# Differential attention: low parts of both maps made in one operation and moved by ScalarE; one maximum for two maps that share a bank

## The chip, the cores and the metric

The kernel runs on one core of a Trainium2 chip. The core has a matrix engine (TensorE, PE in the profile; its weight loads are shown apart as PEld), VectorE (DVE), ScalarE (ACT), GpSimd (POOL), and SyncE (SP), which issues most of the DMAs. Each engine works through its own queue in order; semaphores make one wait for another. SBUF is the on-chip memory; PSUM holds the results of matmuls in eight banks of 128 partitions x 512 f32. The metric is device time in microseconds (us) of one execution. Beside the timed runs there is one profiled execution, with the times of every instruction.

## The reference, cut to what matters

The model is a trunk of two layers, over 512 tokens of width 1024. Each layer has a half-step SwiGLU, a token mixer, a cross-attention into 256 memory tokens, and another half-step SwiGLU, each followed by a layer norm. The mixer of the first layer is the differential attention that the change touches: eight heads, each with two query/key pairs of 64 dimensions (the two "maps"), whose softmaxes are subtracted.

```python
q, k, v = jnp.split(x @ w_qkv, 3, axis=-1)
q = q.reshape(B, S, H, 2, dk)            # H = 8, dk = 64, S = 512
k = k.reshape(B, S, H, 2, dk)
v = v.reshape(B, S, H, 2 * dk)
q = rope(q, c5, s5)
k = rope(k, c5, s5)
...
s = jnp.einsum('bqhcd,bkhcd->bhcqk', qblk, k).astype(jnp.float32) * scale
s = jnp.where(mask, s, jnp.finfo(jnp.float32).min)
p = jax.nn.softmax(s, axis=-1)
a = p[:, :, 0] - lam * p[:, :, 1]
return jnp.einsum('bhqk,bkhe->bqhe', a.astype(v.dtype), v)
```

## The kernel before

Everything is f32. The matmuls take a reduced f32 type (`fp32r`), so each operand is cut in two: a high part, which is a cast by ACT (lines 119, 272, 1046), and a low part, which is what the cast lost, subtracted by DVE (lines 120, 274, 1047). A product is then three matmuls: high x high, high x low, low x high (lines 202 to 204).

**The attention stage.** `da_main` goes through the heads in pairs. For each pair it projects the values, and for each head of it the query and the key, as a tile of 128 rows (64 of the first map, 64 of the second) by 512 tokens. The weights come by DMA, are cut in two by ACT and DVE, and five buffers of each part hold them ahead of TensorE. Beside this main work runs a side chain, `da_side`, for each head and each block of 128 query tokens (i = 0 to 3; block i sees n = 128 (i + 1) keys): scores and softmax (`da_scores`); two steps later the transposes of the difference of the maps (`da_turn`, lines 482, 119, 120); three steps later the product with the values (`da_out`, lines 1092 and 1093), then the sums of squares (lines 1097 to 1101); and at the end of a head the scaling (line 1117, with a factor that POOL makes) and the turn of the output (`da_turn_out`, lines 124, 125). `weave` mixes the two in the order of the program: it counts nominal nanoseconds of the main work and takes a step of the side chain whenever enough have passed. A head's first scores may come 6000 nominal ns after its key's projection. The order on PE follows the program; on ACT and DVE a planner with a cost model may pull operations that are ready ahead of others.

**Query and key.** `da_rope` rotates the projected tile: DVE shuffles it into a tile `t2` (line 1019) and multiplies by the cosines into `t1` (1020), POOL multiplies `t2` by the sines (1021), DVE adds the two (1022). Both tiles are of the tag `rt`, which has two buffers. Then the high and low parts go to where the score matmuls want them. A query of map m is one tile of 128 rows: its high part in the 64 rows of the map, its low part in the other 64. `da_query` makes each half with operations on 64 rows: ACT makes the high part (1032), DVE the low part, written into the other rows (1033); twice each. A key has, for each map, a tile with the high part in both halves, and a tile with the low part in the map's half and zeros in the other. `da_key` makes for each map the high part by ACT (1046), the low part by DVE (1047), and copies the high part to the other half by ACT (1048).

**Scores.** For each map three matmuls go into a PSUM bank: query x high key (1061), query x low key (1062), and the causal mask (1063). Then DVE takes the maximum of each map's rows (1066), ACT exponentiates and sums (1067), DVE takes a reciprocal and a factor (1070, 1071) and subtracts the second map from the first (1072).

**Banks.** `aux` (line 186) gives a bank to each of these tiles (`sc` for scores, `pt` for transposes, `po` for outputs) from three names in rotation, with two buffers for each name, six banks in all; the other two belong to the projections. A tile waits until one of the two buffers of its name has been read to the end. In `da_side` a head draws 8 banks for scores, 4 for transposes, 2 for outputs and 1 for the output's turn, 15 in all.

Of the kernel before, what the change touches and what calls it, by code (L numbers as in the profile page):

```python
# [9 lines left out]
F32 = mybir.dt.float32  # L10
F32R = mybir.dt.float32r
I32 = mybir.dt.int32
AF = mybir.ActivationFunctionType
ALU = mybir.AluOpType
AX = mybir.AxisListType
# [4 lines left out]
S = 512  # L20
# [20 lines left out]
HALVES = (slice(0, DA_DK), slice(DA_DK, P))  # L41
# [68 lines left out]
class Trunk:  # L110
# [72 lines left out]
    def mm(self, name):  # L183
        return self.mmp.tile([P, S], F32, tag="mm", name=name)
# [840 lines left out]
    def da_query(self, ps):  # L1025

        nc, t = self.nc, self.da_rope(ps)
        got = [self.act("qk") for m in range(2)]
        scale = DA_DK**-0.5
        for m, q in enumerate(got):  # L1030
            here, there = HALVES[m], HALVES[1 - m]
            nc.scalar.activation(q[here], t[here], AF.Copy, scale=scale)
            nc.vector.scalar_tensor_tensor(
                q[there], t[here], scale, q[here].bitcast(F32), ALU.mult, ALU.subtract
            )
        return got

    def da_key(self, ps):


        nc, t = self.nc, self.da_rope(ps)
        his, los = [self.act("qk") for m in range(2)], self.low_keys[len(self.heads) % 2]
        for m in range(2):
            here, there = HALVES[m], HALVES[1 - m]
            hi, lo = his[m], los[m]
            nc.scalar.copy(hi[here], t[here])
            nc.vector.tensor_sub(lo[here], t[here], hi[here].bitcast(F32))
            nc.scalar.copy(hi[there], hi[here].bitcast(F32))
        return his, los

    def da_scores(self, st, i):

        nc = self.nc
        q, k, n = st["q"], st["k"], (i + 1) * P
        qi, kn = slice(i * P, n), slice(0, n)
        mx, rc, cf = self.small("mx"), self.small("rc", (P, 1)), self.small("cf", (P, 1))
        sm = st["sm"][:, i]
        sc = [self.aux("sc")[:, :n] for m in range(2)]
        mm = nc.tensor.matmul
        for m in range(2):  # L1060
            mm(sc[m], q[m][:, qi], k[0][m][:, kn], start=True, stop=False)
            mm(sc[m], q[m][:, qi], k[1][m][:, kn], start=False, stop=False)
            mm(sc[m][:, n - P :], self.identr, self.maskr, start=False, stop=True)
        p = [self.tmp("p")[:, :n] for m in range(2)]
        for m in range(2):
            nc.vector.tensor_reduce(mx[:, m : m + 1], sc[m], AX.X, ALU.max, negate=True)
            nc.scalar.activation(
                p[m], sc[m], AF.Exp, bias=mx[:, m : m + 1], accum_out=sm[:, m : m + 1]
            )
        nc.vector.reciprocal(rc, sm[:, 1:2])  # L1070
        nc.vector.scalar_tensor_tensor(cf, sm[:, 0:1], self.nlam, rc, ALU.mult, ALU.mult)
        nc.vector.scalar_tensor_tensor(p[0], p[1], cf, p[0], ALU.mult, ALU.add)
        st["p", i] = p[0]
# [512 lines left out]
```

## Time and profile before

| | us |
|---|---|
| median of the three runs | 1948.64 |
| lowest, highest run | 1948.03, 1959.1 |
| the profiled execution, its own time | 1954.6 |
| its span, from the first to the last instruction | 1952.8 |
| TensorE, VectorE, ScalarE, GpSimd busy | 1917.3, 1567.3, 1019.6, 323.2 |

The profiled execution took 6 us more than the median; durations below come from it. A row of an instruction gives its start in us from the span's start, its length in us, the engine, the line of the kernel, the operation, the tiles that it writes and reads, and, in brackets, how long its engine stood idle before it and what ended that. Matmuls overlap their neighbours, and their ends are modelled; the distance between two starts says more than the length shown. A row of a group gives the line, the engine, the operation, output and input tiles, their shape, the count, then the busy time in us and the mean ns of one, and the idle time before them. A row of a wait names who waited, for whom, the us in total, how often, and the longest. The granted clock of TensorE was 0.994 of full speed over the span.

### The profile page before, as it was taken

To read this page: it belongs to the slowest core of one execution; us is meant where nothing else is said; L and a number is where in the kernel's file an instruction comes from. 1 tells how busy PE (TensorE), PEld (TensorE's weight loads), DVE (VectorE), ACT (ScalarE), POOL (GpSimd) and SP (SyncE) were. 2 spreads that over 40 slices of the span, in tenths; PEclk is the share of its full clock that TensorE was granted. 3 is DMA by queue.
4 is the path that set the end of the run, shared out by engine and by line. 5 is a ranking of instruction groups with operands and counts; after the bars stand their busy time and mean duration, and the time that the engine had idled before them with its cause. 6 is when DMAs were issued, how large, how long until landed. Compare 5 with 4: busy or idle time off the path is not lost.

```text
span 1952.8 us, 32548 instructions
## 1 busy us (share of the span) xinstructions
PE 1917.3 (98%) x13122; PEld 1751.0 (90%) x13122; DVE 1567.3 (80%) x2214; ACT 1019.6 (52%) x1549; POOL 323.2 (17%) x299
## 2 busy tenths in 40 slices
PE   8999999999999999999999999999999999999998
PEld 8999998888778888999998999999888889999996
DVE  6898889788867557889887888888777559988886
ACT  6555454566655434655553655545445336555552
POOL 2112111111211002211220311212100003111211
PEclk9999999999999999999999999999989999999999
DMA  9878772322134316977785687877253338878861
GB/s 272 182 169 178 173 137 76 89 74 78 45 118 140 109 65 183 184 175 161 145 191 170 114 179 162 184 171 142 77 173 130 103 108 151 175 164 170 183 134 56
DMA packets 247031, 277.96 MB, mean 142 GB/s; under 512 B 8288, under 2 KB 212576, under 8 KB 246880
## 3 DMA queue, kind: packets, MB, share of 16 engines
q0 software_dynamic: 92928, 92.29, 30.9%
q1 hardware_dynamic: 153952, 183.59, 29.3%
q8 instruction: 103, 1.69, 0.3%
q14 instruction: 48, 0.39, 0.1%
HBM read 273.75 MB, written 2.10 MB: 141 GB/s over the span
## 4 chain that ended last, share of the span: by engine, by line
PE 50%; DVE 6%; issue 3%; ACT 1%; POOL 1%; DMA 0%; SPq 0%; DVEq 0%; POOLq 0%; ACTq 0%
PE x L202 5%; PE x L203 5%; PE x L204 5%; PE z L202 3%; PE z L204 3%; PE z L203 3%; PE ps L202 2%; PE ps L204 2%; PE ps L203 2%; PE px L202 2%; PE px L204 2%; PE px L203 2%; DVE wl L120 1%; PE y L204 1%; PE x L674 1%
## 5 line engine op out<-in xcount | busy, mean ns | idle before, releaser
L659 POOL DMA_DIRECT2D ra<-in_ffn_w_in_dram x132 | 170.4, 1304 | 996.2 <-DVE wl L120 819.6
L119 ACT CAST wh<-ra 128x1024 fp32r<-128x1024 f32 x184 | 193.5, 1053 | 224.3 <-PE x L203 65.3
L120 DVE TENSOR_TENSOR wl<-ra,wh 128x1024 fp32r<-128x1024 f32 x184 | 223.8, 1220 | 73.8 <-ACT wh L119 73.3
L119 ACT CAST wh<-rc 128x1024 fp32r<-128x1024 f32 x136 | 143.1, 1053 | 119.1 <-PE x L203 38.8
L202 PE MATMUL x<-xe,wh 128*128 128x256 f32 x704 | 195.0, 277 | 0.0
L203 PE MATMUL x<-xe,wh 128*128 128x256 f32 x704 | 194.8, 277 | 0.0
L204 PE MATMUL x<-xe,wl 128*128 128x256 f32 x704 | 194.8, 277 | 0.0
L120 DVE TENSOR_TENSOR wl<-rc,wh 128x1024 fp32r<-128x1024 f32 x136 | 164.6, 1219 | 28.5 <-ACT wh L119 28.0
L119 ACT CAST wh<-b 128x1024 fp32r<-128x1024 f32 x112 | 117.8, 1052 | 131.1 <-PE x L203 65.9
L120 DVE TENSOR_TENSOR wl<-b,wh 128x1024 fp32r<-128x1024 f32 x112 | 136.7, 1220 | 40.2 <-ACT wh L119 40.2
L202 PE MATMUL x<-xh,wh 128*128 128x256 f32 x544 | 151.2, 278 | 0.9 <-DVE hr L738 0.9
L203 PE MATMUL x<-xl,wh 128*128 128x256 f32 x544 | 150.7, 277 | 0.0
L204 PE MATMUL x<-xh,wl 128*128 128x256 f32 x544 | 150.7, 277 | 0.0
L203 PEld LDWEIGHTS x<-xe,wh 128*128 128x128 f32 x704 | 132.5, 188 | 1.4
L202 PEld LDWEIGHTS x<-xe,wh 128*128 128x128 f32 x704 | 132.1, 188 | 1.3
L204 PEld LDWEIGHTS x<-xe,wl 128*128 128x128 f32 x704 | 132.2, 188 | 0.0
L120 DVE TENSOR_TENSOR wl<-raw,wh 128x1024 fp32r<-128x1024 f32 x64 | 80.5, 1265 | 55.1 <-ACT wh L119 54.4
L202 PEld LDWEIGHTS x<-xh,wh 128*128 128x128 f32 x544 | 102.1, 188 | 1.8 <-issue 1.1
L203 PEld LDWEIGHTS x<-xl,wh 128*128 128x128 f32 x544 | 102.5, 188 | 0.7
L119 ACT CAST wh<-raw 128x1024 fp32r<-128x1024 f32 x64 | 66.6, 1049 | 69.2 <-PE xq L203 21.6
L204 PEld LDWEIGHTS x<-xh,wl 128*128 128x128 f32 x544 | 102.2, 188 | 0.0
L204 PE MATMUL y<-xh,wl 128*128 128x256 f32 x352 | 98.4, 280 | 1.5 <-DVE wl L120 0.3
(435 smaller groups left out, 6356.8 us busy)
## 6 DMA issues: line engine op xcount, KB each, us to landing
ra<-in_ffn_w_in_dram POOLq DMA_DIRECT2D x132, 512.0 KB, 6.9
rc<-in_ffn_w_in_dram SPq DMA_DIRECT2D x88, 512.0 KB, 5.9
b<-in_ffn_w_out_dram SPq DMA_DIRECT2D x76, 512.0 KB, 4.9
ra<-in_ffn_w_in_dram SPq DMA_DIRECT2D x44, 512.0 KB, 5.1
rc<-in_ffn_w_in_dram POOLq DMA_DIRECT2D x44, 512.0 KB, 7.8
raw<-in_xa_wkv_dram SPq DMA_DIRECT2D x16, 1024.0 KB, 5.4
raw<-in_da_w_qkv_dram SPq DMA_DIRECT2D x16, 512.0 KB, 5.1
raw<-in_xa_wq_dram SPq DMA_DIRECT2D x8, 1024.0 KB, 5.1
```

What stands on the lines that cost most here:

```text
L119: self.nc.scalar.copy(hi, src),
L120: self.nc.vector.tensor_sub(lo, src, hi.bitcast(F32)),
L202: mm(out, w[0], x[0], start=start, stop=False, skip_group_check=again)
L203: mm(out, w[0], x[1], start=False, stop=False, skip_group_check=again)
L204: self.last_mm = mm(out, w[1], x[0], start=False, stop=stop, skip_group_check=again)
L659: nc.gpsimd.dma_start(t, source(*block), accum_op=ALU.add)
L674: self.last_mm = nc.tensor.matmul(ps[:, j], v[i][:, k, j * P : (j + 1) * P], x[l][:, k], start=n == i == l == 0, stop=n == 7 and i == 1, s ...
```

## The change

A query's low part is made for both maps by one DVE operation of 128 rows, into a third tile of the tag `rt`, and so is its high part by one ACT operation. Three ACT copies of 64 rows then put the pieces where the matmuls want them: the second map's high part and both low parts. A key gets the same: one high part, one low part, then five ACT copies (three of high parts, two of low parts).

In `da_scores`, where both maps' scores fit into one bank (2n up to 512, so blocks 0 and 1), they share one, and DVE takes the maxima of both maps with one operation. A head draws 13 banks then. Blocks 2 and 3 stay as they are.

```diff
 def da_query(self, ps):
         nc, t = self.nc, self.da_rope(ps)
         got = [self.act("qk") for m in range(2)]
         scale = DA_DK**-0.5
-        for m, q in enumerate(got):
-            here, there = HALVES[m], HALVES[1 - m]
-            nc.scalar.activation(q[here], t[here], AF.Copy, scale=scale)
-            nc.vector.scalar_tensor_tensor(
-                q[there], t[here], scale, q[here].bitcast(F32), ALU.mult, ALU.subtract
-            )
+        low = self.tmp("rt")
+
+        self.split_scaled(got[0], low, t, scale)
+        nc.scalar.copy(got[1][HALVES[1]], got[0][HALVES[1]].bitcast(F32))
+        for m in range(2):
+            nc.scalar.copy(got[m][HALVES[1 - m]], low[HALVES[m]])
         return got
...
 def da_key(self, ps):
         his, los = [self.act("qk") for m in range(2)], self.low_keys[len(self.heads) % 2]
-        for m in range(2):
-            here, there = HALVES[m], HALVES[1 - m]
-            hi, lo = his[m], los[m]
-            nc.scalar.copy(hi[here], t[here])
-            nc.vector.tensor_sub(lo[here], t[here], hi[here].bitcast(F32))
-            nc.scalar.copy(hi[there], hi[here].bitcast(F32))
+        low = self.tmp("rt")
+        self.split(his[0], low, t)
+        for half in HALVES[::-1]:
+            nc.scalar.copy(his[1][half], his[0][HALVES[1]].bitcast(F32))
+        nc.scalar.copy(his[0][HALVES[1]], his[0][HALVES[0]].bitcast(F32))
+        for lo, half in zip(los, HALVES):
+            nc.scalar.copy(lo[half], low[half])
         return his, los
...
 def da_scores(self, st, i):
-        sc = [self.aux("sc")[:, :n] for m in range(2)]
+        both = 2 * n <= S
+        if both:
+            sc = self.aux("sc")[:, : 2 * n].rearrange("p (m n) -> p m n", m=2)
+            pair, sc = sc, [sc[:, m] for m in range(2)]
+        else:
+            sc = [self.aux("sc")[:, :n] for m in range(2)]
...
+        if both:
+            nc.vector.tensor_reduce(mx, pair, AX.X, ALU.max, negate=True)
         for m in range(2):
-            nc.vector.tensor_reduce(mx[:, m : m + 1], sc[m], AX.X, ALU.max, negate=True)
+            if not both:
+                nc.vector.tensor_reduce(mx[:, m : m + 1], sc[m], AX.X, ALU.max, negate=True)
             nc.scalar.activation(
```

## The prediction

> **What bounds the kernel now.** I read the page first, then the stage that the change touches, stretch by stretch, then the waits of TensorE in that stage.
>
> ```profile
> span 1952.8 us, 32548 instructions
> PE 1917.3 (98%) x13122; PEld 1751.0 (90%) x13122; DVE 1567.3 (80%) x2214; ACT 1019.6 (52%) x1549; POOL 323.2 (17%) x299
> ```
>
> The second row is busy time by engine over the whole span. TensorE (PE) is covered at 98%, VectorE (DVE) at 80%, ScalarE (ACT) at 52%. These are means over eight stages, so the attention stage is read by itself. Its head loop lies between 362 and 580 us. In the rows below the columns after the length are PE, PEld (weight loads), DVE, ACT and POOL in us busy, then the granted clock, DMA share and GB/s.
>
> ```profile
> 362.00:580.00 218.00, 213.20 (x1257) 177.89 (x1256) 176.86 (x372) 135.72 (x363) 35.89 (x48) 1.00 0.26 79
> ...
> 460.00:480.00 20.00, 19.61 (x104) 16.25 (x103) 17.99 (x38) 14.34 (x38) 5.48 (x7) 1.00 0.33 106
> 480.00:500.00 20.00, 18.36 (x98) 14.09 (x98) 15.88 (x36) 12.78 (x34) 4.26 (x6) 1.00 0.16 53
> 500.00:520.00 20.00, 18.64 (x106) 14.50 (x104) 16.90 (x34) 12.07 (x35) 5.60 (x7) 1.00 0.16 54
> 520.00:540.00 20.00, 19.70 (x145) 17.69 (x145) 16.87 (x39) 15.55 (x46) 2.05 (x4) 1.00 0.18 56
> ```
>
> TensorE is uncovered for 218.00 - 213.20 = 4.8 us of this stage, and 3.4 of those fall between 460 and 540 us, the later heads. That is all that a change of DVE and ACT work can win here, unless the covered time itself hides stalls. The starts of three neighbouring projection matmuls say that it mostly does not:
>
> ```profile
> 501.80 0.39 PE L202 MATMUL q<-xh,wh 128*128 128x512 f32 x1
> 502.04 0.39 PE L203 MATMUL q<-xl,wh 128*128 128x512 f32 x1
> 502.27 0.39 PE L204 MATMUL q<-xh,wl 128*128 128x512 f32 x1
> ```
>
> They start 0.23 to 0.24 us apart, although each is shown 0.39 long: an uninterrupted stream. So TensorE bounds the stage, and what counts is where it stops:
>
> ```profile
> PE sc L1061 <- DVE a L120: 1.7, 2, 1.3
> PE pt L482 <- ACT o L1117: 1.1, 1, 1.1
> PE po L1092 <- ACT a L119: 0.6, 1, 0.6
> PE sc L1061 <- ACT po L1101: 0.6, 1, 0.6
> PE po L1093 <- DVE a L120: 0.3, 1, 0.3
> PE pt L482 <- ACT p L1067: 0.2, 1, 0.2
> ```
>
> Columns: us in total, times, longest. The two `sc` rows, 1.7 + 0.6 = 2.3 us, are score matmuls that wait for a PSUM bank still being read. The largest one:
>
> ```profile
> 498.80 0.39 PE L1061 MATMUL sc<-qk 128*128 128x256 f32 x1 [1.31 <-DVE a L120]
> ```
>
> It has 256 columns, so it is query block 1, and it is the second map's, since the first map's had started before it. Blocks 0 and 1 are those whose maps will share a bank.
>
> **The change part by part.** The durations, from the groups by shape (busy us, mean ns of one, idle before):
>
> ```profile
> L1033 DVE SCALAR_TENSOR_TENSOR qk<-rt,qk 64x512 fp32r<-64x512 f32 x16 | 11.0, 686 | 1.2 <-ACT qk L1032 0.7
> L1047 DVE TENSOR_TENSOR low<-rt,qk 64x512 fp32r<-64x512 f32 x16 | 10.9, 684 | 0.4
> L120 DVE TENSOR_TENSOR qk<-raw,qk 128x512 fp32r<-128x512 f32 x4 | 2.7, 684 | 0.0
> L1032 ACT ACTIVATE qk<-rt 64x512 fp32r<-64x512 f32 x16 | 10.1, 630 | 12.1 <-DVE rt L1022 11.9
> L1048 ACT CAST qk<-qk 64x512 fp32r<-64x512 f32 x16 | 9.9, 619 | 0.4
> L119 ACT CAST qk<-raw 128x512 fp32r<-128x512 f32 x4 | 2.5, 616 | 0.0
> L1066 DVE TENSOR_REDUCE mx<-sc 128x1 f32<-128x512 f32 x16 | 10.3, 681 | 1.2 <-PE sc L1063 1.2
> L1066 DVE TENSOR_REDUCE mx<-sc 128x1 f32<-128x256 f32 x16 | 6.2, 416 | 0.5 <-PE sc L1063 0.5
> L1066 DVE TENSOR_REDUCE mx<-sc 128x1 f32<-128x128 f32 x16 | 4.0, 279 | 0.0
> ```
>
> *Low parts.* 64 partitions cost what 128 do: 684 and 684 ns on DVE, 619 and 616 on ACT. A query or key therefore loses one of its two DVE subtractions: 8 heads x (686 + 684) = 11.0 us off DVE. On ACT a query goes from 2 operations to 4 and a key from 4 to 6: 8 x 4 x 0.619 = 19.8 us more. ACT goes from 135.7 to 155.5 of 218, DVE from 176.9 down. No DMA, no matmul and no POOL operation moves.
>
> *Maxima.* Per head, block 0 turns 2 x 279 into about one 416 (256 elements, the nearest row), block 1 turns 2 x 416 into about one 681. The saving is 8 x (142 + 151) = 2.3 us of DVE; bounds for the two-row form, which the trace does not show, are one single maximum (8 x (279 + 416) = 5.6 saved) and two (nothing). I take the rows of equal element count. DVE together: 13.3 us less, beside TensorE, so worth nothing by itself.
>
> *Bank use.* A head draws 13 banks from the rotation in place of 15, over three names with two buffers each. The second map of blocks 0 and 1 needs no bank any more, so the 2.3 us of `sc` waits above should go. But the neighbours of every other tile in the rotation change. Counting the order of the code: the output tile `po` of blocks 2 and 3 used to follow two `sc` tiles of its name, long read; now it follows the `pt` of the output turn and the `po` of blocks 0 and 1. It waits until DVE L125 or the second ACT L1101 square is over. What the trace has for these moments:
>
> ```profile
> 429.64 0.19 ACT L1101 ACTIVATION_READ_ACCUMULATOR po<-o 128x1 f32 x1
> 430.48 0.28 PE L1092 MATMUL po<-v,a 128*128 128x256 f32 x1
> ...
> 502.50 0.28 PE L1092 MATMUL po<-v,a 128*128 128x256 f32 x1
> 502.97 0.74 DVE L125 SCALAR_TENSOR_TENSOR oT<-pt,subg,oT 128x512 fp32r<-128x512 f32 x1
> 503.13 0.19 ACT L1101 ACTIVATION_READ_ACCUMULATOR po<-o 128x1 f32 x1
> ...
> 526.70 0.29 PE L1092 MATMUL po<-v,a 128*128 128x256 f32 x1
> 526.84 0.19 ACT L1101 ACTIVATION_READ_ACCUMULATOR po<-o 128x1 f32 x1
> ```
>
> Around 430 the bank would be free 0.65 us early; around 503 it would come 0.8 late, around 527 some 0.3 late. Since TensorE arrives there sooner by the `sc` waits of 498.80 and of head 5 (1.3 and 0.6), those two gains are given back, and 1.1 us is lost on top. Only the third `sc` wait (1.7 - 1.3 = 0.4) is a clear gain.
>
> *Longer ACT chains.* A key's ACT chain grows by 2 x 0.62 = 1.25 us, and the low copies wait for DVE's subtraction; behind them on ACT stand the next weight cast, exponentials and squares, and for those wait DVE L1070, the transposes and `po`. The first score matmul follows the key at once in two heads:
>
> ```profile
> 420.89 0.62 ACT L1048 CAST qk<-qk 64x512 fp32r<-64x512 f32 x1
> 421.93 0.22 PE L1061 MATMUL sc<-qk 128*128 128x128 f32 x1
> ...
> 468.58 0.62 ACT L1048 CAST qk<-qk 64x512 fp32r<-64x512 f32 x1
> 469.47 0.22 PE L1061 MATMUL sc<-qk 128*128 128x128 f32 x1
> 469.69 0.31 PE L1061 MATMUL sc<-qk 128*128 128x128 f32 x1
> ```
>
> Slack 0.42 and 0.27 us; the last copy is the second map's, needed some 0.25 later. Stalls: 1.25 - 0.42 - 0.25 = 0.6 and 1.25 - 0.27 - 0.25 = 0.7, together 1.3. Bounds: nothing, if DVE reaches the rotary sums 0.69 earlier for the subtraction that it no longer does in the query before; and 1.3 + 2.5 if the query's two extra copies push both keys as well. The query's 1.25 also lands just before the squares that free `po`: 0.6 us lost around 430 (1.25 against the slack of 0.65), and between 0 and 1.25 around 503, where ACT is often idle; I take 0.6.
>
> [...] The two maps' first matmuls start 0.22 us apart (469.47, 469.69). [...] The joint maximum waits for all six matmuls anyway, and the second exponential, which sets L1070, starts no later than now, so the sum keeps zero.
>
> *Sum*: -2.3 (`sc` waits) + 1.9 (given back) + 1.1 (`po` late) + 1.2 (query copies before `po`) + 1.3 (keys) = +3.2 us; DVE's relief may take back about 0.7 at one of the two keys: +2.5 us. The profiled execution took 1954.6, so 1957.1 for its like; it lies 6 us above the median of the runs, 1948.64, and its stalls are the best that I have for that too: 1948.6 + 2.5 = 1951.
>
> **The rivals.**
> *DVE's relief wins.* All waits on DVE and on `sc` banks go (1.7 + 0.6 + 0.3 = 2.6 us) and nothing comes for them: 1946.0; with the ACT waits too, 4.8: 1943.8. For it: DVE is the fuller engine, 18.0 of 20 us in 460 to 480. Against it: the four slacks above.
> *ACT makes `po`'s bank late in every head* (slower). If the 2.5 us that each head adds on ACT all reach the squares, the loss is 2.5 less the slack of about 0.7 in five heads and 2.5 + 0.5 in two: 9.0 + 6.0, halved where ACT idles beside it, some 8 to 15 us: 1957 to 1964. It decides from an ACT load near that of 520 to 540: 15.6 + 2.5 of 20. Against it: the other stretches have 12 to 14.
> *The relief does not happen*: `low` is a third tile in the two buffers of `rt`, so the next head's shuffle, which starts DVE's rotary work, must wait for ACT's copies.
>
> ```profile
> 469.16 0.75 DVE L1019 STREAM_SHUFFLE rt<-q 128x512 f32<-128x512 f32 x1
> ```
>
> It started just as the key's last copy ended (469.20); 1.25 later means DVE blocked 1.25 in each of 7 heads, 8.8 us at most: 1957.4. Against it: TensorE does not need that query for another head's time.
> *TensorE is not the bound.* Weight loads cover 177.89 of 218 us, 82%. [...] With TensorE 18% free, VectorE's chain would set the stage and its 13.3 us come off: 1935.3. The matmul starts 0.23 us apart speak against it.
>
> **How the numbers follow.** Forecast 0.50 (1949 to 1954), relief wins 0.24, ACT late 0.17, no relief 0.06, TensorE not the bound 0.03. A change of 1% is 19.5 us, about what a measurement of this kernel can tell from none: hardly any case reaches it, so within 1% has 0.94; slower 0.04 is the tail where ACT's whole 19.8 us show, faster 0.02 the last rival with more. The range of 1945 to 1959 leaves out the far end of the relief (some 0.1) and the upper part of the ACT cases (some 0.1).
>
> **What would show it.** In the attention stage: 16 operations fewer at the low parts and 16 at the maxima on DVE, 32 more on ACT; ACT 20 us busier, DVE 13 less; no `sc` wait of TensorE at blocks 0 and 1; new waits at L1092's line for DVE `oT` or ACT `po`, and at the first scores for an ACT copy. TensorE's uncovered time should be 6 to 9 us in place of 4.8. Wrong would be: an uncovered time under 3 us, a run of ACT waits in every head, or a change outside of this stage.

## The result and the profile after

The changed kernel is slower by 0.3%: over 22 runs each the medians are 1951.68 us before and 1958.96 us after, the ratio is 1.0032 with a 95% interval of 1.0021 to 1.0043, which is 6.2 us (4.1 to 8.4); the two medians themselves lie 7.3 us apart. The kernel before had shown 1948.64 in three runs; its median over 22 is 3.0 us higher.

The head of the page of the changed kernel, span and busy time of each engine:

```profile
span 1956.3 us, 32565 instructions
PE 1913.4 (98%) x13122; PEld 1746.0 (89%) x13122; DVE 1551.1 (79%) x2182; ACT 1039.1 (53%) x1581; POOL 326.0 (17%) x299
```

DVE has 32 instructions and 16.2 us less than before, ACT 32 more and 19.5 us more. TensorE still covers 98%. The profiled execution took 1958.09 us, only 3.5 more than the one of before; that one had 17 us at half clock in a later stage (last section), which this one had not. So I compare the attention stage, not the span. Its stretches, in the columns of the prediction (length; PE, PEld, DVE, ACT, POOL busy; clock; DMA share; GB/s):

```profile
362.00:580.00 218.00, 209.90 (x1229) 175.27 (x1228) 159.60 (x335) 154.66 (x394) 36.32 (x48) 0.98 0.24 75
520.00:530.50 10.50, 7.62 (x64) 7.13 (x62) 7.89 (x15) 9.42 (x26) 2.56 (x4) 1.00 0.00 1
531.00:537.50 6.50, 6.25 (x27) 5.64 (x28) 3.48 (x10) 2.96 (x10) 0.00 (x0) 0.50 0.00 1
538.00:545.00 7.00, 7.00 (x51) 6.09 (x50) 3.44 (x6) 3.49 (x10) 1.24 (x2) 1.00 0.13 19
```

TensorE is uncovered for 218.00 - 209.90 = 8.1 us in place of 4.8. Of 520 to 530.5 it misses 2.9 us, while ACT is busy 9.42 of 10.5. In the 6.5 us that follow it is covered, but at a granted clock of 0.50: 27 matmuls, where the next 7 us hold 51. Both come after the last of the eight keys. TensorE's waits between 362 and 586 us (us in total, times, longest):

```profile
PE po L1101 <- ACT po L1110: 3.8, 2, 3.6
PE po L1101 <- ACT a L119: 1.6, 2, 1.1
PE po L1102 <- DVE a L120: 1.3, 2, 0.7
PE pt L482 <- ACT o L1126: 1.1, 1, 1.1
```

No wait for a bank of `sc` is left. In its place the first output product of blocks 2 and 3 (L1101, L1092 before) waits once for 3.6 us, for ACT's squares. The end of that wait, in order of time (start, length, engine, line):

```profile
524.55 0.62 ACT L119 CAST qk<-rt 128x512 fp32r<-128x512 f32 x1 [1.00 <-DVE rt L1022]
525.54 1.25 ACT L1046 CAST qk<-qk 64x512 fp32r<-64x512 f32 x2
526.82 0.62 ACT L1049 CAST low<-rt 64x512 fp32r<-64x512 f32 x1
527.45 0.62 ACT L1047 CAST qk<-qk 64x512 fp32r<-64x512 f32 x1
528.08 0.61 ACT L1049 CAST low<-rt 64x512 fp32r<-64x512 f32 x1
528.70 0.37 ACT L1076 ACTIVATE p<-sc,mx 128x128 f32<-128x128 f32 x1
529.07 0.36 ACT L1106 COPY o<-po 128x256 f32<-128x256 f32 x1
530.35 0.29 ACT L1110 ACTIVATE po<-o 128x128 f32<-128x128 f32 x1
530.79 0.28 ACT L1110 ACTIVATE po<-o 128x128 f32<-128x128 f32 x1
531.25 0.58 PE L1101 MATMUL po<-v,a 128*128 128x256 f32 x1 [3.61 <-ACT po L1110]
```

These are ACT's rows for the key and the bank, with others left out, and the matmul that waits. The key's high part comes first, then its five copies, one behind the other; behind them the second map's exponential, the copy of an output tile (L1106), a turn of the output (L124), an exponential of block 1 and the two squares that write into that tile's bank. Only with the last square is the bank free, 3.6 us after TensorE was ready for it. The key of before, at the same place:

```profile
522.06 1.26 ACT L1046 CAST qk<-rt 64x512 fp32r<-64x512 f32 x2 [0.58 <-DVE rt L1022]
523.34 1.26 ACT L1048 CAST qk<-qk 64x512 fp32r<-64x512 f32 x2
```

Four operations there, 522.06 to 524.60, or 2.5 us; here six, 524.55 to 528.69, or 4.1. The longer chain is 1.6 us of the wait. As much again comes from its start: the key is 524.55 - 522.06 = 2.5 us later than before, while TensorE is ready only 0.9 later, at 531.25 - 3.61 = 527.64 in place of 526.70 (its row in the prediction). With the 0.3 us by which this bank would have been late already, that makes 3.5. In the trace the key starts late because its rotary sum (L1022) does, at 523.84 in place of 521.34: POOL's product for it (L1021) starts at 521.36 in place of 517.89, since POOL was busy until then with the factor of an output, and this had waited for squares that stood on ACT between and behind the query's new copies. So the query's copies have a share in it too; this is read from one trace and was not tried alone.

How long the stage is, from its first query matmul to its last output matmul. These are the rows of the query's and of an output's matmul, before (first two) and after; after the count stand the shortest, median and longest in ns, then the first and the last start:

```profile
L202 PE MATMUL q<-xh,wh x64: 393/398/507, 350.4 to 504.8; 128*128 128x512 f32 x64
L1093 PE MATMUL po<-v,a x80: 220/223/327, 388.6 to 567.6; 128*128 128x128 f32 x80
```

```profile
L202 PE MATMUL q<-xh,wh x64: 393/398/507, 351.6 to 507.0; 128*128 128x512 f32 x64
L1102 PE MATMUL po<-v,a x80: 220/223/330, 390.3 to 575.2; 128*128 128x128 f32 x80
```

567.6 - 350.4 = 217.2 before, 575.2 - 351.6 = 223.6 after: 6.4 us more, about the difference of the runs. In the second stretch of half clock the projection matmuls of 128x256 start 0.21 to 0.22 us apart (533.12, 533.34, 533.55), and just behind it 0.11 to 0.12 (538.00, 538.11, 538.23). So I take half clock to cost half its length, an estimate from these starts: 3.4 us of it lie in the stage before (near its start), 3.4 + 6.8 after. Without it the stage takes 217.2 - 1.7 = 215.5 and 223.6 - 5.1 = 218.5. **So 3.0 us are stops of TensorE, and 3.4 are the slower clock behind the longest stop.**

### The profile page after: what moved, and what is told of

It reads as the page before. It is cut to its first block, busy times and chain, and to the rows that moved or that the text cites. A ratio compares the mean times of both kernels' runs of the same rounds, so it can differ in the third digit from the quotient of the medians.

```text
span 1956.3 us, 32565 instructions
## 1 busy us (share of the span) xinstructions
PE 1913.4 (98%) x13122; PEld 1746.0 (89%) x13122; DVE 1551.1 (79%) x2182; ACT 1039.1 (53%) x1581; POOL 326.0 (17%) x299
## 4 chain that ended last, share of the span: by engine, by line
PE 50%; DVE 6%; issue 3%; ACT 1%; DMA 1%; POOL 1%; SPq 0%; DVEq 0%; POOLq 0%; ACTq 0%
PE x L202 5%; PE x L203 5%; PE x L204 5%; PE z L202 3%; PE z L204 3%; PE z L203 3%; PE ps L202 2%; PE ps L204 2%; PE ps L203 2%; PE px L204 2%; PE px L202 2%; PE px L203 2%; DVE wl L120 1%; PE y L204 1%; PE x L674 1%
## 5 line engine op out<-in xcount | busy, mean ns | idle before, releaser
L119 ACT CAST wh<-ra 128x1024 fp32r<-128x1024 f32 x184 | 193.4, 1053 | 227.0 <-PE x L203 59.1
L120 DVE TENSOR_TENSOR wl<-ra,wh 128x1024 fp32r<-128x1024 f32 x184 | 224.0, 1222 | 76.8 <-ACT wh L119 76.3
L119 ACT CAST wh<-rc 128x1024 fp32r<-128x1024 f32 x136 | 143.1, 1053 | 118.1 <-PE x L203 38.7
L119 ACT CAST wh<-b 128x1024 fp32r<-128x1024 f32 x112 | 117.8, 1051 | 130.9 <-PE x L203 67.2
L120 DVE TENSOR_TENSOR wl<-rc,wh 128x1024 fp32r<-128x1024 f32 x136 | 164.9, 1222 | 28.0 <-ACT wh L119 27.8
L120 DVE TENSOR_TENSOR wl<-b,wh 128x1024 fp32r<-128x1024 f32 x112 | 136.9, 1223 | 40.2 <-ACT wh L119 40.2
L120 DVE TENSOR_TENSOR wl<-raw,wh 128x1024 fp32r<-128x1024 f32 x64 | 80.4, 1259 | 55.5 <-ACT wh L119 54.9
L119 ACT CAST wh<-raw 128x1024 fp32r<-128x1024 f32 x64 | 66.8, 1051 | 67.3 <-PE xq L203 23.5
```

The costliest lines, as they stand in the source:

```text
L119: self.nc.scalar.copy(hi, src),
L120: self.nc.vector.tensor_sub(lo, src, hi.bitcast(F32)),
```

## The experiments

Each kernel is measured in two ways. The stage is taken as above, from one profiled execution, with its half clock (in us) and the length without that. The ratio is that of all runs. The last column does the same correction to the runs: the mean time, less (1 - granted clock) x 1950 us, against that of the kernel before on the same chip. It is an estimate from the clocks listed with the runs. The scatter of the runs gives this column a standard error of 0.5 to 1.1 us, so that differences under 2 us say little in it; two executions of the change gave stages of 218.5 and 218.3 without half clock. For the changed kernel itself the runs of before beside it list no clocks; there the values that the other runs of before gave (1943.3 to 1944.1) stand for them.

| kernel | stage | half clock | without | ratio [95%] | runs, without |
|---|---|---|---|---|---|
| before | 217.2 | 3.4 | 215.5 | 1 | 0 |
| the change | 223.6 | 10.2 | 218.5 | 1.0032 [1.0021, 1.0043] | +3.7 to +4.5 |
| e_low | 219.1 | 6.8 | 215.7 | 0.9990 [0.9977, 1.0003] | +0.5 |
| e_max | 215.7 | 0 | 215.7 | 0.9997 [0.9982, 1.0013] | +2.3 |
| e_rot | 219.9 | 3.4 | 218.2 | 1.0013 [0.9995, 1.0031] | +3.3 |
| e_max_rot | 215.7 | 0 | 215.7 | 0.9994 [0.9979, 1.0010] | -0.2 |
| e_q | 215.5 | 0 | 215.5 | 1.0002 [0.9986, 1.0019] | -0.7 |
| e_k | 222.5 | 6.8 | 219.1 | 1.0031 [1.0012, 1.0049] | +4.8 |
| e_skipb | 221.6 | 6.8 | 218.2 | 1.0029 [1.0012, 1.0046] | +2.8 |
| e_pool | 218.0 | 3.4 | 216.3 | 0.9998 [0.9980, 1.0016] | +1.5 |
| e_first | 220.3 | 6.8 | 216.9 | 1.0035 [1.0023, 1.0047] | +2.9 |
| e_first_rot | 215.5 | 3.4 | 213.8 | 0.9997 [0.9980, 1.0014] | -2.4 |
| e_best | 214.05 | 0 | 214.05 | 0.9984 [0.9964, 1.0005] | -1.5 |

**The two halves of the change, one at a time.** Only the low parts (`da_query` and `da_key` as changed, `da_scores` as before, 15 banks a head):

```diff
-        both = 2 * n <= S
-        if both: ...
-        else:
-            sc = [self.aux("sc")[:, :n] for m in range(2)]
+        sc = [self.aux("sc")[:, :n] for m in range(2)]
```

> Low parts side by side and moved by ScalarE, but scores and maxima as before (15 banks a head, no shared bank). Bank theory: the output tile of blocks 2 and 3 again follows two score tiles, so TensorE does not stop there for ScalarE's squares; the score waits of before (2.3 us) stay or grow a little, the clock is not halved in the attention stage; ratio to before 0.9995 to 1.0010. Rival, ScalarE's longer chains by themselves: the loss of the full change stays, ratio 1.0025 to 1.0040.

Only the shared bank and the joint maximum (13 banks a head), with query and key as before:

```diff
-        low = self.tmp("rt")
-        self.split(his[0], low, t)
...
+        for m in range(2):
+            here, there = HALVES[m], HALVES[1 - m]
...
```

> Shared bank and one maximum for blocks 0 and 1, low parts as before (13 banks a head, short ScalarE chains). Bank theory: TensorE waits for the output bank at two or three heads, but for 0.3 to 1 us each and without a halved clock; the score waits of blocks 0 and 1 are gone; ratio 0.9990 to 1.0010. Rival, ScalarE's longer chains by themselves: no wait for the output bank to speak of, ratio 0.9985 to 0.9995.

For neither is a loss shown. Alone, the low parts leave the stage at 215.7, though with 6.8 us of half clock, which I had not expected there, and the `sc` waits stay, as they should, since its banks are as before (the waits of TensorE for `sc` on DVE in e_low):

```profile
PE sc L1062 <- DVE cf L1072: 1.7, 1, 1.7
PE sc L1062 <- DVE a L120: 1.0, 2, 0.6
```

With the shared bank alone these are gone and `po` waits, though more than the 0.3 to 1 us that I expected of each (e_max):

```profile
PE po L1100 <- ACT a L119: 1.9, 2, 1.0
PE po L1100 <- ACT po L1109: 1.7, 1, 1.7
PE po L1100 <- DVE oT L125: 0.9, 1, 0.9
```

The stage is even again at 215.7. By the stage, the loss therefore belongs to the two halves together. The clock-corrected runs of e_max stand 2.3 above before, the stage only 0.2; that difference I can't place.

**Which bank comes late.** If 13 banks a head put `po` behind the wrong tile, one more step of the rotation, behind each shared bank, gives back the old neighbours:

```diff
             pair, sc = sc, [sc[:, m] for m in range(2)]
+            self.aux_turn += 1
```

This was done to the change (e_rot) and to the shared bank alone (e_max_rot).

> The full change, and where the maps share a bank the rotation of names is moved on by one, so that a head counts 15 again and the output tile of blocks 2 and 3 follows score tiles as before. Bank theory: the waits of TensorE for the output bank on ScalarE's squares (3.8 us in total) are gone, and with them the half clock (6.8 us long) in the attention stage; ratio 0.9990 to 1.0010. Rival, ScalarE's longer chains by themselves: ratio stays at 1.0025 to 1.0040, with TensorE waiting at other places for ScalarE.

> Shared bank and one maximum, low parts as before, and the rotation moved on by one so that a head counts 15. Bank theory: no output bank wait and no score wait of blocks 0 and 1, so the best of the four: ratio 0.9980 to 0.9995 (2.3 us less is 0.9988). Rival: the same as without the moved rotation, 0.9985 to 0.9995.

The waits of `po` for ACT's squares did vanish in e_rot, but not the loss: its stage is 218.2 without half clock. (Its ratio alone, 1.0013 with an interval that reaches 0.9995, would not decide.) The stop stands elsewhere: the transposes wait for ACT's exponentials four times, 5.7 us in all, and longest for 3.0. The end of that wait, in order of time:

```profile
524.08 0.74 DVE L1082 SCALAR_TENSOR_TENSOR p<-p,cf 128x512 f32<-128x512 f32 x1
529.59 0.37 ACT L1077 ACTIVATE p<-sc,mx 128x128 f32<-128x128 f32 x1
530.11 0.66 PE L482 MATMUL pt<-ident,p 128*128 128x128 f32 x4 [2.99 <-ACT p L1077]
```

The data of these transposes were there at 524.82. What they waited for is the bank: it was the one shared by two maps, and the second map's exponential, which reads it last, stood on ACT behind the key's copies and ended at 529.96. So the theory that the rotation alone is to blame falls. The move changes which tile waits for that stretch of ACT. In e_max_rot, whose key stands on ACT as before, no stop is longer than 1.1 us, and its stage is no better than that of e_max.

**Query or key.** The change with the key as before (e_q), and with the query as before (e_k); each puts the loop over the maps back into one of the two functions:

```diff
 def da_key(self, ps):      # e_q; e_k: the same in da_query
-        low = self.tmp("rt")
-        self.split(his[0], low, t)
...
+        for m in range(2):
+            here, there = HALVES[m], HALVES[1 - m]
...
```

> The full change with the key as before: only the query's low part is made side by side; shared bank for blocks 0 and 1. Theory now: what stops TensorE is a bank that ScalarE must still read while the second exponential and the squares stand behind a key's five copies, and a shared bank is held longer than two; so with the key's old chain of four no stop over 2 us; first query matmul to last output matmul 215.5 to 217.5 us without a halved clock (before 217.2 with 3.4 us of it); ratio 0.9985 to 1.0010. Rival, ScalarE's total load: a part of the loss in proportion stays, 1.0010 to 1.0020.

> The full change with the query as before: only the key's low part is made side by side; shared bank for blocks 0 and 1. Theory now: the stop of 3 to 4 us for an output bank stays at the last key but one; stage 217.5 to 220 us without and 3 more with a halved clock; ratio 1.0010 to 1.0035. Rival, ScalarE's total load: no stop over 2 us, 1.0010 to 1.0020.

The key's copies are enough for the loss: without them the stage is at 215.5 and the ratio 1.0002; with them and the query as before, 219.1 and 1.0031. TensorE's longest wait, first of e_q, then of e_k:

```profile
PE po L1100 <- ACT po L1109: 1.9, 1, 1.9
```

```profile
PE po L1101 <- ACT po L1110: 4.0, 2, 2.9
```

In e_k the wait at the last key is 2.9 us and not 3.6, which fits the query's share above. The 1.9 us of e_q are another wait for squares, at 502 us; e_max, with the old query and key, waits there 1.7, so this one comes from the 13 banks, and costs about what the removed `sc` waits give back. At the last key e_q waits 1.0 us, for DVE's L125. (The expectations place the wait at the last key but one; by the rows above it is the last one.)

**Another place for the extra step.** The rotation moved on ahead of the shared bank instead of behind it, so that the maps share another bank:

```diff
         if both:
+            self.aux_turn += 1
             sc = self.aux("sc")[:, : 2 * n].rearrange("p (m n) -> p m n", m=2)
```

> The full change, with the rotation moved on by one before the shared bank instead of behind it: the shared banks then stand in other names than the next transposes, and the output tile of blocks 2 and 3 finds a long-free neighbour. Theory now: no stop over 2 us for a bank on ScalarE, score waits of about 2 us in total as before; stage 215.5 to 217.5 us without a halved clock; ratio 0.9990 to 1.0010. Rival, ScalarE's total load: stage over 218 us as with the move behind it, 1.0010 to 1.0020.

This expectation failed: 1.0029, with the stage at 218.2. The stops are at the scores now, for banks that DVE still reads or that wait for DVE (e_skipb):

```profile
PE sc L1068 <- DVE a L120: 3.8, 3, 1.8
PE sc L1068 <- DVE cf L1081: 2.0, 1, 2.0
```

Three orders of the rotation, three names for the stop (`po`, `pt`, `sc`), and nearly one price: 218.5, 218.2, 218.2. That the key's copies are behind the stops of e_skipb too isn't shown: the readers there are DVE's.

**The copies off ACT.** All four copies of low parts by GpSimd, in query and key:

```diff
-            nc.scalar.copy(lo[half], low[half])
+            nc.gpsimd.tensor_copy(lo[half], low[half])
```

> The full change with the copies of the low parts by GpSimd instead of ScalarE (two for a query, two for a key). ScalarE's chains are then as long as before and VectorE keeps its relief. Theory now: no stop over 2 us; stage 214.5 to 217 us without a halved clock; ratio 0.9980 to 1.0005. Rival: GpSimd's copies are slow (its multiplication of 128x512 took 1.29 us) and stand behind the rotary product, so first scores wait for them, 0.5 to 2 us in heads 2 and 4: ratio 1.0000 to 1.0020.

The group of these copies, and the waits of TensorE, in e_pool:

```profile
L1049 POOL CAST low<-rt 64x512 fp32r<-64x512 f32 x16 | 9.9, 621 | 25.3 <-DVE rt L120 22.3 <-DVE rc L1079 2.5
```

```profile
PE po L1101 <- ACT po L1110: 1.7, 1, 1.7
PE sc L1067 <- POOL low L1049: 1.4, 1, 1.4
```

GpSimd takes 621 ns for such a copy, ACT 619. The wait of 3.6 us at the last key goes: there TensorE now waits 1.3 us, for DVE's L125, and the 1.7 us for squares are those at 503, as in e_max. No loss is left in the ratio (0.9998). So what stands on ACT ahead of the squares is the cause of the long stop. One first score now waits 1.4 us for GpSimd, the stop that the rival had named; the stage is 216.3, no gain.

**The order on ACT.** Both exponentials put ahead of the key's copies in the planner, with the bank rotation of the change (e_first), and with the step of e_rot as well (e_first_rot):

```diff
+            with self.tc.high_priority():
                 nc.scalar.activation(
                     p[m], sc[m], AF.Exp, bias=mx[:, m : m + 1], accum_out=sm[:, m : m + 1]
                 )
```

> The full change, with the exponentials put ahead in the planner, so that on ScalarE both exponentials of block 0 of the last key but one stand ahead of that key's five copies; the output copy and the squares still stand behind them. Theory (a bank that ScalarE frees only after the key's copies): TensorE's stop for the output bank on the squares stays, 2.5 to 4 us; first query matmul to last output matmul 217.5 to 219.5 us plus half of any halved clock; ratio 1.0010 to 1.0035. Rival, the late second exponential itself was the cause: no stop over 2 us, 215.5 to 217.

> The same, and the rotation moved on by one behind the shared bank (15 a head), where TensorE's stop had been 3.0 us in front of the transposes, because they took the bank that the second exponential still read. Theory: that exponential now stands ahead of the key's copies, so this stop goes and no stop over 2 us is left; 215.5 to 217.5 us plus half of any halved clock; ratio 0.9990 to 1.0012. Rival, ScalarE's total load: 218 us and more, 1.0010 to 1.0020.

This tells a late exponential from late squares. In e_first the squares still stand behind the key, but the wait there is smaller than the 2.5 to 4 us expected: 1.7, and it ends with DVE's L125, which waited for ACT's turn of the output (L124) behind the key's copies. The other one is that for squares near 503 (the two longest waits of e_first):

```profile
PE po L1102 <- ACT po L1111: 1.8, 1, 1.8
PE po L1102 <- DVE oT L125: 1.7, 1, 1.7
```

In e_first_rot the tile that waits is one whose last reader is the exponential, which is early now; no long stop is left (the longest wait of e_first_rot):

```profile
PE po L1103 <- ACT a L119: 1.5, 1, 1.5
```

It has every operation of the change, ACT's 20 us too, and its stage takes 213.8, 1.7 less than before. With the same extra step but the old order on ACT (e_rot) it is 218.2. So the loss isn't ACT's load but what stands behind the key on ACT, and for which bank. No run puts the exponentials first in the kernel before, so how much of the 1.7 us that order would win by itself is open. e_first itself contradicts a part of this: its stage is only 1.4 over before, yet its runs are at 1.0035. Their mean clock is 0.9933 against 0.9960 of the runs of before beside them, (0.9960 - 0.9933) x 1950 = 5.3 us; why its clock is granted so is open.

**The change once more**, to see whether the half clock behind the stop comes again:

> The changed kernel once more, for one look at TensorE's clock. If the halved clock of 6.8 us belongs to the stop of 3.6 us at 527 to 531 us, it comes again at the same place; if it falls where it likes, as in the pooling stage, it does not, and the stage takes 220 us in place of 223.6.

The wait in this execution of the changed kernel:

```profile
PE po L1101 <- ACT po L1110: 3.6, 1, 3.6
```

Half clock follows it from 530.3 for 6.8 us (granted clock 0.50 over 530.5 to 537.0 us, 1.00 over 538 to 545). Stop, half clock and stage (223.4, 218.3 without) are as in the first.

**A version from both findings:** the shared bank with the extra step, the exponentials first, and the low parts as before, so that ACT gets nothing more to do:

```diff
             pair, sc = sc, [sc[:, m] for m in range(2)]
+            self.aux_turn += 1
...
+            with self.tc.high_priority():
                 nc.scalar.activation(
```

> Shared bank and one maximum for blocks 0 and 1, the rotation moved on by one behind it, exponentials ahead in the planner, low parts as before. The parts that shortened the attention stage are together, and the key's long chain on ScalarE is out. Theory: fewest stops; first query matmul to last output matmul 213 to 215.5 us without a halved clock, 1 to 3 us less than before; ratio 0.9975 to 0.9995. Rival: the longer key chain is no cost once the exponentials stand ahead, so this is no better than the full change with both corrections: ratio 0.9990 to 1.0005.

1950.46 us against 1951.84, ratio 0.9984 with an interval that reaches 1.0005: the lowest ratio here, but not shown to beat the kernel before. Its stage (214.05) is not better than that of e_first_rot (213.8), so in these two executions the low parts side by side cost nothing once the order on ACT is right, and win at most a few tenths of a microsecond.

## Why the prediction was right or wrong

The measured 1958.96 is 8.0 us above the forecast of 1951. It lies outside the 1949 to 1954 that the forecast's own case was given, and inside the range of 1945 to 1959 by 0.04 us, which is luck. 3.0 of the 8.0 us are the base: 1948.64 from three runs stands at 1951.68 over 22. The rest is the sum: +2.5 forecast, +6.2 by the ratio, or +7.3 between the medians. Slower by less than 1% was right, and so was what bounds the stage; the size of the main loss was not. Point by point:

- **TensorE bounds the stage: right.** DVE lost 16.2 us and the stage grew. DVE's relief went into waiting: its reciprocals waited for the exponentials for 30.3 us in place of 16.0 (before first, after second).

```profile
DVE rc L1070 <- ACT p L1067: 16.0, 15, 2.7
```

```profile
DVE rc L1079 <- ACT p L1076: 30.3, 21, 2.7
DVE rt L1020 <- ACT low L1049: 3.8, 3, 1.6
```

- **Sizes of the operations: right.** The groups of the changed kernel by shape:

```profile
L1049 ACT CAST low<-rt 64x512 fp32r<-64x512 f32 x16 | 9.9, 619 | 0.3
L1072 DVE TENSOR_REDUCE mx<-sc 128x2 f32<-128x512 f32 x8 | 5.5, 682 | 0.5 <-PE sc L1069 0.5
L1072 DVE TENSOR_REDUCE mx<-sc 128x2 f32<-128x256 f32 x8 | 3.3, 416 | 0.0
```

  A maximum of two rows took what one of as many elements had taken before: 416 ns for 256 elements (416), 682 for 512 (681). Together 8 x (416 + 682) = 8.8 us, 2.3 less than 8 x 2 x (279 + 416) = 11.1, as reckoned. ACT got 19.5 us, reckoned 19.8. DVE lost 16.2, reckoned 13.3; the last section says where the other 2.9 are.
- **The `sc` waits go (-2.3): right**, none is left.
- **Stalls at a key's first scores (+1.3): too high.** The waits of the weight loads for the key's copies are 0.7 and 0.3:

```profile
PEld sc L1067 <- ACT qk L1047: 0.7, 2, 0.5
PEld sc L1068 <- ACT low L1049: 0.3, 2, 0.2
```

- **`po` late (0.8 at 503, 0.3 at 527): the step that failed, by its size.** Kind, engine and place were right: the output tile of blocks 2 and 3 waits for the squares at about 527. But 0.3 us became 3.6. I had shifted the end of the squares of before against TensorE's arrival, and added the query's two copies to the stretches at 430 and 503, but nothing to that at 527. There the last key stands on ACT ahead of the squares: its chain grew from 2.5 to 4.1 us, and it started later against TensorE by another 1.6. The sum had both copies of the query and copies of the key, but no term for either at this place.
- **The query's copies before `po` (0.6 at 430, 0.6 at 503), and 0.8 at 503: too high.** At 430 TensorE doesn't wait, and at 505 it waits 0.2 us for the squares. In place of that, waits of outputs for L119 and L120 (1.6 and 1.3 us) came, which the sum didn't have. The uncovered time, 8.1 us, came out within the 6 to 9 forecast because errors of both signs met; that is luck.
- **A term was missing:** half clock after the stop, 3.4 us of the 6.4 by which the stage grew.
- **The rivals.** "ACT makes `po`'s bank late" gave the time and named the load from which it decides, that of 520 to 540, and there it struck; but in one head and not in every one. It had reckoned 1.8 to 3.0 us in each of seven heads, halved; one head lost 3.6 us of stop and 3.4 by half clock, and 3.0 came from the base. That its 1957 to 1964 holds the measured time is therefore luck. "The relief does not happen" is seen as a wait of DVE for the third `rt` tile, 3.8 us in three places, beside TensorE's path. "Relief wins" needs the order of e_first_rot, where the stage did gain 1.7 us; in the runs that gain isn't shown (0.9980 to 1.0014). "TensorE isn't the bound" is refuted by 16.2 us of DVE that bought nothing.
- **The shared bank (zero in the sum): right for the joint maximum.** No run shows a cost of it on TensorE's path: e_max_rot's stage is 0.2 us over that of before and e_best's below it, and DVE's idle time ahead of the joint maxima is 0.5 us in all (above). What the shared bank does cost is another thing: it is held until the later of two readers, and in e_rot, where that one stood on ACT behind a key's copies, the next tile waited 3.0 us.

## What to carry to other kernels

Work moved to an engine with idle time isn't free if the operations that release a busy engine's buffers are queued behind it (here ACT, busy for 52% of the span before, and 3.0 us of stops): look not at its share of busy time, but at what stands behind the moved work in its queue at the fullest place, and reckon the whole chain there, its start too, not the added part against an old slack. If a stop only changes its name when buffers are handed out in another order, look for the late reader before the order, and put the releasing operations ahead. A stop of TensorE can be paid for twice: here the longest took 3.6 us, and the 6.8 us behind it, at a granted clock of 0.50, are reckoned at 3.4 more.

## What was not expected of the hardware

- **The clock was halved behind some stops in mid-kernel.** The stretches at a granted clock of 0.50 are 3.4 us long or a multiple: 3.4 near the start of the stage in seven of the kernels, 6.8 behind the 3.6 us stop of the change, in both executions, and 6.8 behind 2.9 us in e_k, but none behind the 3.0 us of e_rot (granted clock 1.00 over 530.5 to 537.0 us). Kernels whose longest stop was 1.5 to 2.0 us differ: over 480 to 540 us the granted clock is 0.97 in e_low, e_skipb, e_first and e_first_rot, which is 3.4 us at half clock, and 1.00 in e_max, e_q and e_pool with 1.7 to 1.9. The length of a stop alone didn't decide. In the traces of before and of the change the beginnings of the stretches lie whole multiples of 3.413 us apart: 353.30 and 530.79 in the change, 52 of them, and 351.88 and 1427.08 before, 315. I cut both traces from 14 to 1935 us into pieces of this length that start or end where a stretch begins. Four pieces at full clock have half clock behind them; TensorE is uncovered in them for 1.84 and 1.92 us (before) and for 1.83 and 3.15 (the change). In no other piece is it uncovered for more than 1.62. Two neighbouring pieces over the stop of e_rot, and one ahead of the half clock of e_k (the columns as above; the first two rows are e_rot, the third is e_k):

```profile
525.03:528.44 3.41, 2.08 (x18) 1.81 (x16) 3.41 (x6) 2.93 (x7) 0.00 (x0) 1.00 0.00 0
528.44:531.85 3.41, 1.75 (x16) 1.75 (x16) 1.74 (x6) 3.35 (x11) 0.00 (x0) 1.00 0.00 0
526.00:529.41 3.41, 1.18 (x11) 0.98 (x9) 1.73 (x5) 3.37 (x10) 0.00 (x0) 1.00 0.00 0
```

  TensorE is uncovered for 1.33 and 1.66 us in the two pieces of e_rot, and for 2.23 in that of e_k; only the last is followed by half clock. This was read off the traces afterwards, and no run moved a stop to test whether the uncovered part of such a piece is what decides. How long half clock then lasts isn't explained.
- **It was halved behind two short waits as well.** The profiled execution of before had half clock in the later pooling stage too. Ahead of it stand two waits of only 0.87 and 1.06 us, in one such piece, which has 1.92 us uncovered (first row; the second is the half clock):

```profile
1423.66:1427.08 3.42, 1.50 (x11) 1.10 (x10) 3.36 (x7) 3.13 (x5) 0.00 (x0) 1.00 1.07 361
1427.00:1444.00 17.00, 16.91 (x79) 16.91 (x80) 12.59 (x18) 8.82 (x13) 0.00 (x0) 0.50 0.33 108
```

  By half of 17 us this makes a single profiled execution 8.5 us longer, more than the change itself. Of the two profiled executions of the changed kernel, the first has none at this place (full clock from 537.6 to 1950.7 us). The second's granted clock over its span of 1960.3 us was 0.992, which makes 2 x (1 - 0.992) x 1960 = 31 us at half clock, an estimate; 10.2 of them lie in the stage. Stages have to be compared, or many runs.
- **Operations that nobody touched got shorter.** The subtractions for the weights' low parts on DVE, before and after:

```profile
L274 DVE TENSOR_TENSOR wl<-raw,wh 128x512 fp32r<-128x512 f32 x24 | 19.7, 832 | 0.2
```

```profile
L274 DVE TENSOR_TENSOR wl<-raw,wh 128x512 fp32r<-128x512 f32 x24 | 16.0, 690 | 0.8 <-ACT wh L272 0.8
```

  3.7 us less in one group, which more than covers the 2.9 us by which DVE's fall exceeded the reckoning. The cause wasn't tried.
